# Row fetches, gate matrix layout and modulation sums in a two-layer block with PEER experts

## The chip, the cores and the metric

The kernel runs on one core of a Trainium2 chip, in one launch. The metric is the device time of one execution in microseconds; the shown time is the median of three runs. Five engines take part: TensorE (PE; its weight loads are PEld), VectorE (DVE), ScalarE (ACT), GpSimd (POOL) and SyncE (SP), which here mainly issues DMAs. Each engine works through its own list of instructions in order; semaphores hold an instruction until what it needs is there.

## The reference

Two blocks in a row on x of 256 tokens by 1024, in float32. The first has two layers of [mixer, PEER expert layer], each with adaptive norms; the second, a twice repeated [swiglu, hybrid mixer, swiglu], isn't touched by the change. What matters here is the first block:

```python
def first_block(...):
    for layer in range(2):
        sh1, sc1, g1, sh2, sc2, g2 = split(cond @ ada_w[layer] + ada_b[layer], 6)      # 1024 x 6144
        csh1, csc1, cg1, csh2, csc2, cg2 = split(cond_ctx @ ada_w[layer] + ada_b[layer], 6)
        h, hc = modulate(rmsnorm(x), sh1, sc1), modulate(rmsnorm(ctx), csh1, csc1)
        y, yc = even_mixer(h, hc) if layer == 0 else odd_mixer(h, hc)                  # MLA
        x = x + g1 * y
        x = x + g2 * peer_ffn(modulate(rmsnorm(x), sh2, sc2), ...)
        if layer == 0:
            ctx = ctx + cg1 * yc
            ctx = ctx + cg2 * peer_ffn(modulate(rmsnorm(ctx), csh2, csc2), ...)

def peer_ffn(h, w_q, sub_keys, u_tab, v_tab):       # 128 x 128 experts, 8 heads, 16 chosen per head
    s = einsum(h @ w_q, sub_keys)                   # scores against two sets of 128 keys
    expert, gate = top16 of the sums of the two top-16 lists; gate = softmax
    act = gelu(einsum('td,thkd->thk', h, u_tab[expert]))
    return einsum('thk,thkd->td', gate * act, v_tab[expert])
```

The twelve modulation vectors of a layer (shift, scale and gate for the mixer and for the expert layer, each for x and for the context) are sums over the 1024 rows of ada_w. In layer 1 the context is wanted only as input of the mixer, so of the context's vectors only the first two are used there.

## The kernel before

Tokens lie in tiles of 128: layer 0 has four (two of x, two of the context), layer 1 two. Every float32 product is three matmuls of a high and a low part (L311, L312, L313, the helper `mm3`); a weight slab is cast on ScalarE (L342, `wh`) and its rest is taken on VectorE (L316, `wl`). All elementwise helpers have one line each: L316 two tensors, L325 multiply and add with a column (`stt`), L320 a tensor and a scalar.

**PEER layer.** `peer_route` computes scores, the top 16 and a dense gate matrix: for every token its weight for each of the 16384 experts. `gbuild` makes it for 32 tokens at a time in a staging tile (tag T16: two of them in layer 0, one in layer 1; ScalarE writes it at L1310) and L1314 writes it to DRAM, 2 MB per 32 tokens, 12 writes in layer 0 and 8 in layer 1. It is laid out as [32-token block][row][all experts]. Beside it, twelve of the 32 chunks get their hidden part u made ahead (`pre`, 1, 4, 6, 9, 12, 14, 17, 20, 22, 25, 28, 30) and stored in `ud`. Then come the chunks of 512 experts: u_part multiplies the tokens by a chunk of the u table (or reads `ud`), applies the gate, for which the chunk's slice of the gate matrix is read back at L1376 (`t<-gd`, 768 KB in layer 0, 512 KB in layer 1), and v_tiles multiplies by the chunk of the v table. V of chunk c-1 follows U of chunk c.

**Layer 0** (`peer_mixed`, 950 to 1885 us) does three token tiles so, 384 columns wide. The fourth, tile 0, is done by fetching rows: 128 steps fetch for each token one row of the u table (`pur`, L1442 on GpSimd, an indirect DMA of 512 KB) and multiply it by the token's vector on VectorE (L1447); 128 steps fetch rows of the v table (`pvr`) and add them up (L325, 128x1024). The fetches share five buffers (tag GR). A counter (`rate`) says after how many matmul groups the next fetch is written.

**Modulation sums.** `ada_thread` makes them 512 columns at a time: an accumulator is cleared on GpSimd (L470), the bias is loaded into its first row (L472), eight pieces of ada_w of 128x512 are multiplied by a column of the condition and added on VectorE (L325, 128x512), for x and the context, and TensorE sums over the partitions (L308). In layer 0's chunks stand the fourteen blocks that are left by then: columns 10 and 11 of layer 0, and all twelve of layer 1, 56 loads of 512 KB (L1586). Blocks 4 to 11 of layer 1 only need x, so one sum per piece.

**What follows.** `tail` adds a finished token tile to the residual (loaded at L1595, `t<-rd`) and makes the norm of layer 1. The first projection of MLA follows (`mwa`, `mwb`, result `pm`), then the attention by heads (scores, softmax on VectorE and ScalarE with L607 and L609, values) and the output projection (`mwo`), then route 1, and the dense chunks of layer 1 (`peer_dense`).

**The order.** The program's text sets dependences and priorities, but a list scheduler fixes each engine's order ahead of the run; pools of buffers (`T4`, `raw`, `GR`) limit how early a load may stand. DMAs on SP are in one queue list: a load that waits for a buffer holds all later ones.

## Time and profile before

| | us |
|---|---|
| median of three runs (4143.91 to 4156.93) | 4145.16 |
| profiled execution | 4154.18 |
| its span, first to last instruction | 4152.4 |
| TensorE busy | 3949.9 (95%) |
| VectorE busy | 2978.3 (72%) |
| ScalarE busy | 1910.5 (46%) |
| GpSimd busy | 748.4 (18%) |

Stages on its time axis: layer 0's mixer to about 627 us, its route to 950, its chunks with row fetches to about 1885, the transition with the first projection to 1965, the attention and output projection to 2065, route 1 to 2300, the dense chunks of layer 1 to 2860, the second block to the end. A share of busy time is a mean over stages: TensorE's 95% says that most stages wait for it, and the windows say which do not. An idle engine matters only where TensorE waits for it.

### The profile page before, as it was taken

Reading aid. Unit: us, or ns where it says so; the run is one execution under the profiler, and the core shown is the slowest. Engines: PE = TensorE matmul, PEld = TensorE weight load, DVE = VectorE, ACT = ScalarE, POOL = GpSimd, SP = SyncE. Lnnn points to the kernel's source line nnn. Section 1 sums busy time; section 2 is a strip of 40 time slices with the busy share of each in tenths; the row PEclk is TensorE's granted clock in tenths of the full one; section 3 lists DMA queues with packets and bytes.
Section 4 is the critical chain, followed back from the end, with each engine's and each line's share of the span. In section 5 each row is a group of like instructions: output and inputs, shape, how many; then the busy total and the mean of one; then the engine's idle time right before and its main releaser. Section 6 shows DMA issues by size and latency. Waiting matters only on the chain.

```text
span 4152.4 us, 63830 instructions
## 1 busy us (share of the span) xinstructions
PE 3949.9 (95%) x24927; PEld 3558.4 (86%) x24927; DVE 2978.3 (72%) x5618; ACT 1910.5 (46%) x3241; POOL 748.4 (18%) x579
## 2 busy tenths in 40 slices
PE   8999999998999999999999999999999999999999
PEld 5877888897888778888789988888989998989988
DVE  4468579986998889847699556656667766567765
ACT  3344344772333233335558544444554454444444
POOL 2133302113444556300131000000010000000000
PEclk9999999999999999999999999999999999999999
DMA  4222133669999999843247866665545455445443
GB/s 169 92 84 79 44 141 111 221 253 327 353 363 353 354 373 369 328 162 123 97 162 277 288 221 227 242 221 190 182 169 188 179 178 178 173 168 183 174 172 142
DMA packets 234974, 862.66 MB, mean 208 GB/s; under 512 B 18944, under 2 KB 116096, under 8 KB 164528
## 3 DMA queue, kind: packets, MB, share of 16 engines
q1 hardware_dynamic: 197808, 724.35, 49.0%
q0 software_dynamic: 36864, 134.23, 8.5%
q8 instruction: 195, 3.19, 0.3%
q14 instruction: 107, 0.88, 0.1%
HBM read 795.97 MB, written 62.55 MB: 207 GB/s over the span
## 4 chain that ended last, share of the span: by engine, by line
PE 54%; DVE 16%; DMA 8%; issue 3%; ACT 1%; POOL 1%; SPq 0%; DVEq 0%; POOLq 0%; ACTq 0%
PE p L311 17%; PE p L313 17%; PE p L312 17%; DVE t L316 5%; DVE t L325 4%; DVE wl L316 3%; DMA t<-in_pvr,c 2%; DMA w<-in_pv 2%; DMA t<-in_ada_w 2%; PE p L308 2%; DVE t L1447 1%; PE p L435 1%; POOL t L1442 1%; DMA w<-ud 1%; DMA t<-in_pur,c 0%
## 5 line engine op out<-in xcount | busy, mean ns | idle before, releaser
L316 DVE TENSOR_TENSOR wl<-w,wh 128x1024 fp32r<-128x1024 f32 (+1 forms) x933 | 1132.1, 1219 | 704.7 <-ACT wh L342 682.6
L342 ACT CAST wh<-w 128x1024 fp32r<-128x1024 f32 x1017 | 1057.8, 1047 | 999.8 <-PE p L312 430.0
L311 PE MATMUL p<-t,wh 128*128 128x256 f32 (+2 forms) x4784 | 1460.1, 305 | 17.9 <-ACT wh L342 4.5
L313 PE MATMUL p<-t,wl 128*128 128x256 f32 (+2 forms) x4784 | 1450.1, 303 | 5.2 <-DVE wl L316 3.3
L312 PE MATMUL p<-t,wh 128*128 128x256 f32 (+2 forms) x4784 | 1449.5, 303 | 1.4 <-DVE t L316 1.4
L311 PEld LDWEIGHTS p<-t,wh 128*128 128x128 f32 x4784 | 921.7, 193 | 39.1 <-ACT wh L342 6.9
L313 PEld LDWEIGHTS p<-t,wl 128*128 128x128 f32 x4784 | 921.5, 193 | 19.3 <-DVE wl L316 5.1
L312 PEld LDWEIGHTS p<-t,wh 128*128 128x128 f32 x4784 | 921.9, 193 | 17.0 <-DVE t L316 1.7
L312 PE MATMUL p<-wl,t 128*128 128x512 f32 (+3 forms) x2134 | 818.0, 383 | 25.7 <-DVE wl L316 24.8
L311 PE MATMUL p<-wh,t 128*128 128x512 f32 (+3 forms) x2134 | 817.8, 384 | 21.6 <-ACT t L401 11.4
L313 PE MATMUL p<-wh,t 128*128 128x512 f32 (+3 forms) x2134 | 815.0, 383 | 8.0 <-DVE t L316 6.1
L316 POOL TENSOR_TENSOR wl<-w,wh 128x1024 fp32r<-128x1024 f32 x84 | 220.2, 2632 | 1983.1 <-ACT wh L342 1714.0
L312 PEld LDWEIGHTS p<-wl,t 128*128 128x128 f32 x2134 | 410.3, 192 | 100.8 <-DVE wl L316 29.9
L311 PEld LDWEIGHTS p<-wh,t 128*128 128x128 f32 x2134 | 409.9, 192 | 100.3 <-ACT t L401 13.8
L313 PEld LDWEIGHTS p<-wh,t 128*128 128x128 f32 x2134 | 408.2, 192 | 89.4 <-DVE t L316 10.8
L316 DVE TENSOR_TENSOR t<-t,t 128x256 f32<-128x256 f32 (+10 forms) x732 | 352.9, 487 | 64.6 <-ACT t L401 42.3
L325 DVE SCALAR_TENSOR_TENSOR t<-t,c,t 128x512 f32<-128x512 f32 (+2 forms) x367 | 328.1, 920 | 44.9 <-DMA t<-in_ada_w 20.9
L401 ACT CAST t<-t 128x256 fp32r<-128x256 f32 (+3 forms) x314 | 138.7, 446 | 363.4 <-DVE t L316 363.4
L308 PE MATMUL p<-t,t 128*128 128x128 f32 (+3 forms) x1536 | 226.0, 301 | 1.9 <-DVE t L325 1.9
L1442 POOL DMA_INDIRECT t<-in_pvr,c x128 | 199.2, 1556 | 156.2 <-DVE t L325 127.7
L1442 POOL DMA_INDIRECT t<-in_pur,c x128 | 171.4, 1339 | 240.4 <-DVE c L1447 198.5
L308 PEld LDWEIGHTS p<-t,t 128*128 128x128 f32 (+1 forms) x1536 | 193.1, 192 | 25.0 <-issue 11.3
(200 smaller groups left out, 3004.5 us busy)
## 6 DMA issues: line engine op xcount, KB each, us to landing
w<-in_pu SPq DMA_DIRECT2D x128, 1024.0 KB
w<-in_pv SPq DMA_DIRECT2D x128, 1024.0 KB
w<-in_fgu SPq DMA_DIRECT2D x88, 1024.0 KB
w<-in_hin SPq DMA_DIRECT2D x48, 1024.0 KB
w<-in_fdn SPq DMA_DIRECT2D x44, 1024.0 KB
gd<-t SPq DMA_DIRECT2D x20, 2048.0 KB
t<-in_ada_w SPq DMA_DIRECT2D x56, 512.0 KB
t<-gd SPq DMA_DIRECT2D x32, 768.0 KB
```

What stands on the lines that cost most here:

```text
L308: nc.tensor.matmul(o, l, r, start=first, stop=last)
L311: nc.tensor.matmul(o, l[0], r[0], start=first, stop=False)
L312: nc.tensor.matmul(o, l[0], r[1], start=False, stop=False)
L313: nc.tensor.matmul(o, l[1], r[0], start=False, stop=last)
L316: return (e or nc.vector).tensor_tensor(o, a, b, op)
L325: nc.vector.scalar_tensor_tensor(o, a, s, b, op0=op0, op1=op1)
L342: i = nc.scalar.copy(hi[:, :m], raw[:, s : s + m])
L401: nc.scalar.copy(dst[0], src)
L435: nc.tensor.transpose(o, i, ident[:n, :n])
L1442: nc.gpsimd.indirect_dma_start(r, None, src, at)
L1447: nc.vector.tensor_tensor_reduce(r, r, xr, 1.0, 0.0, ALU.mult, ALU.add, act[:, s : s + 1])
```

## The change

Three things change.

1. Of the fourteen blocks of modulation sums in layer 0's chunks only six stay: columns 10 and 11 of layer 0, and 0 to 3 of layer 1. Columns 4 and 5 are made during the first projection of layer 1, 6 to 9 during its attention, 10 and 11 during its dense chunks. In the latter two places the pieces come as loads of 1 MB through the ring of raw weight slabs (`ada_raws`), and the accumulator has a tag of its own (AD).
2. The gate matrix in DRAM is laid out as [chunk][row][32-token block x 128]. A chunk's slice is now one run of 6 KB (layer 0) or 4 KB (layer 1) per partition, where it was twelve or eight runs of 512 B; a write of 32 tokens becomes 32 runs of 512 B per partition, where it was one of 16 KB.
3. The row fetches' rate is reckoned to the end of chunk 31, and what is left of them and the fetched tile's `tail` are written before the last token tile of chunk 31 instead of before the whole of it. One normed tile takes a buffer of tag T6 instead of GR.

```diff
     def ada_thread(blocks, acc_tag, row_tag, raws):
         for l, n, c0 in blocks:
-            acc = T(acc_tag, [P, 2, 512])
-            nc.gpsimd.memset(acc[:, c0:, :], 0.0)
+            a2 = T(acc_tag, [P, 2 - c0, 512])
+            acc = {c: a2[:, c - c0, :] for c in range(c0, 2)}
+            nc.gpsimd.memset(a2, 0.0)
...
+    def ada_raws(l, n):
+        for kh in range(2):
+            w = load(A["ada_w"][l, 2 * n + kh])
+            for k in range(4):
+                yield w[:, k * 512 : (k + 1) * 512]
...
             if g2 == 3:
-                nc.sync.dma_start(gd[tb], st[0].rearrange("p a b -> p (a b)"))
+                o = gd.rearrange("c p (b e) -> b p c e", e=P)[tb]
+                nc.sync.dma_start(o, st[0].rearrange("p (c a) b -> p c (a b)", a=4))
...
-                nc.sync.dma_start(HG[c, "g"], gd[:, :, HS(c)].rearrange("b p e -> p b e"))
+                nc.sync.dma_start(HG[c, "g"], gd[c].rearrange("p (b e) -> p b e", e=P))
...
-    def peer_dense(l, cols, nt, gd, ud, pre):
+    def peer_dense(l, cols, nt, gd, ud, pre, side):
...
+            next(side, None)
             u_part(c, 1)
...
-        rate = 2 * P / (4 + 30 * (4 + 2 * nt)) * 1.0001
+        rate = 2 * P / (4 + 31 * (4 + 2 * nt) + 4) * 1.0001
...
-        for _ in got:
-            pass
-        for n in range(2):
-            tail(0, n, acc0[:, n * 512 : (n + 1) * 512])
         Ws = [v_slab(31, hf) for hf in range(2)]
         for t in range(nt):
+            if t == nt - 1:
+                for _ in got:
+                    pass
+                for n in range(2):
+                    tail(0, n, acc0[:, n * 512 : (n + 1) * 512])
             for hf in range(2):
-                v_tiles(31, hf, Ws[hf], [t])
+                v_tiles(31, hf, Ws[hf], [t], step)
...
-        gd = pdr.tile([12, P, 4096], F32, tag="gd", name="gd0")
+        gd = pdr.tile([32, P, 12 * P], F32, tag="gd", name="gd0")
...
-            ab = [(0, 10, 0), (0, 11, 0)] + [(1, n, n > 3) for n in range(12)]
+            ab = [(0, 10, 0), (0, 11, 0)] + [(1, n, 0) for n in range(4)]
...
+                        hT[t] = Pair("T6" if t else "GR", [P, 8, P]), 0
...
+            ad = ada_thread([(1, n, 1) for n in (4, 5)], "T4", "T2", raws)
...
                     nc.scalar.copy(pm[:, t, c0 : c0 + w], ps[:, :w])
+                    for _ in range(2):
+                        next(ad, None)
...
+        ad = ada_thread([(1, n, 1) for n in range(6, 10)], "AD", "T2", ada_raws)
...
         for h in range(8):
             p = scores(h)
+            next(ad, None)
             if prev is not None:
                 list(attend(h - 1, prev))
+            next(ad, None)
...
-        gd = pdr.tile([8, P, 4096], F32, tag="gd1", name="gd1")
+        gd = pdr.tile([32, P, 8 * P], F32, tag="gd1", name="gd1")
...
-        with phase("D2", T8=4, T4=4):
-            y = dense()
+        with phase("D2", T8=4, T4=4, AD=1):
+            y = dense(ada_thread([(1, n, 1) for n in (10, 11)], "AD", "T2", ada_raws))
```

Where the instructions stand on three engines follows, at the places that matter.

VectorE in layer 0, between the two halves (`wl`) of the same slab of the v table, the 41st, in chunk 20; `t_9004` is the sum of the fetched rows, `t_14091` a modulation sum. Before:

```order
L316 TENSOR_TENSOR wl_13825<-w_13822,wh_13824 128x1024
L325 SCALAR_TENSOR_TENSOR t_9004<-t_14159,c_9084,t_9004 128x1024
L325 SCALAR_TENSOR_TENSOR t_14091<-t_14162,c_78,t_14091 128x512
L325 SCALAR_TENSOR_TENSOR t_9004<-t_14209,c_9084,t_9004 128x1024
L325 SCALAR_TENSOR_TENSOR t_14091<-t_14162,c_78,t_14091 128x512
L325 SCALAR_TENSOR_TENSOR t_9004<-t_14242,c_9084,t_9004 128x1024
L325 SCALAR_TENSOR_TENSOR t_14091<-t_14297,c_78,t_14091 128x512
L316 TENSOR_TENSOR wl_13829<-w_13822,wh_13828 128x1024
```

The same place now:

```order
L316 TENSOR_TENSOR wl_13646<-w_13643,wh_13645 128x1024
L325 SCALAR_TENSOR_TENSOR t_9004<-t_14982,c_9084,t_9004 128x1024
L325 SCALAR_TENSOR_TENSOR t_9004<-t_14997,c_9084,t_9004 128x1024
L325 SCALAR_TENSOR_TENSOR t_9004<-t_15040,c_9084,t_9004 128x1024
L325 SCALAR_TENSOR_TENSOR t_9004<-t_15073,c_9084,t_9004 128x1024
L316 TENSOR_TENSOR wl_13650<-w_13643,wh_13649 128x1024
```

The three multiply-adds of the sums are gone, and a fourth fetched row stands in their place. Over the whole stage the last fetched row is added about when chunk 24's v slabs are split, where it was chunk 26.

SP in the attention of layer 1, its list of DMAs; `in_muq` are weights of the queries, `in_mwo` of the output projection, `in_pq` of route 1. Before:

```order
L334 DMA w_16980<-in_muq 128x1536
L1641 DMA c_16624<-in_rope 128x256
L334 DMA w_17038<-in_muq 128x1536
L334 DMA w_17497<-in_mwo 128x2048
L334 DMA w_17507<-in_mwo 128x2048
L334 DMA w_17593<-in_mwo 128x2048
L334 DMA w_17603<-in_mwo 128x2048
L334 DMA w_17733<-in_pq 128x2048
```

Now, from the second load of muq:

```order
L334 DMA w_16899<-in_muq 128x1536
L334 DMA w_16933<-in_ada_w 128x2048
L334 DMA w_17006<-in_ada_w 128x2048
L334 DMA w_17064<-in_ada_w 128x2048
L334 DMA w_17163<-in_ada_w 128x2048
L473 DMA t_17003<-in_ada_b 1x512
L334 DMA w_17221<-in_ada_w 128x2048
L334 DMA w_17308<-in_ada_w 128x2048
L473 DMA t_17160<-in_ada_b 1x512
L334 DMA w_17366<-in_ada_w 128x2048
L334 DMA w_17433<-in_mwo 128x2048
```

Seven loads of ada_w (the eighth stands before muq) now stand between muq and mwo in the same ring of raw slabs.

VectorE in the attention; the reductions, L609 or L616 (reciprocals) and 128x512 scalings are the softmax of one query tile after the other. Before:

```order
L609 RECIPROCAL t_17111<-t_17109 128x1
L1735 TENSOR_REDUCE t_17120<-p_17114 128x1
L320 TENSOR_SCALAR t_17108<-t_17108,t_17111 128x512
L320 TENSOR_SCALAR t_17122<-t_17120 128x1
L609 RECIPROCAL t_17127<-t_17125 128x1
L1735 TENSOR_REDUCE t_17136<-p_17130 128x1
L320 TENSOR_SCALAR t_17124<-t_17124,t_17127 128x512
```

Now:

```order
L616 RECIPROCAL t_16994<-t_16992 128x1
L1753 TENSOR_REDUCE t_17016<-p_17010 128x1
L320 TENSOR_SCALAR t_16991<-t_16991,t_16994 128x512
L320 TENSOR_SCALAR t_17018<-t_17016 128x1
L325 SCALAR_TENSOR_TENSOR t_17003<-w_17006,c_78,t_17003 128x512 x2
L616 RECIPROCAL t_17023<-t_17021 128x1
L1753 TENSOR_REDUCE t_17032<-p_17026 128x1
L320 TENSOR_SCALAR t_17020<-t_17020,t_17023 128x512
```

Two multiply-adds of the sums now stand ahead of a reciprocal, in the place where VectorE waits for ScalarE's exponentials.

## Rows read from the trace of the kernel before

**Rows 1.** Windows of the stages, core 0; the first row names the columns.
```profile
core 0: us, PE busy (x) PEld busy (x) DVE busy (x) ACT busy (x) POOL busy (x), PEclk, DMA share, GB/s
950.00:1380.00 430.00, 406.71 (x1973) 356.07 (x1972) 387.00 (x588) 139.04 (x192) 183.04 (x140) 0.98 0.96 354
1380.00:1600.00 220.00, 200.75 (x972) 176.28 (x971) 191.35 (x223) 69.25 (x97) 116.31 (x72) 0.97 0.97 366
1600.00:1740.00 140.00, 131.13 (x606) 111.51 (x605) 123.70 (x122) 42.84 (x59) 80.38 (x58) 0.96 0.98 367
1740.00:1885.00 145.00, 145.00 (x714) 129.39 (x714) 68.11 (x84) 53.94 (x73) 0.00 (x0) 1.00 0.49 170
```

**Rows 2.** Chain of waits by line, 1380 to 1600 and 1600 to 1740 us.
```profile
by line: DMA t<-in_ada_w 28.0%; DMA t<-in_pvr,c 17.8%; issue 17.6%; DVE t L325 10.5%; DMA w<-ud 9.0%; DVE wl L316 6.3%; POOL t L1442 6.2%; DVE t L316 5.2%; DVE w L316 2.3%; POOL t L470 0.4%; DVE t L320 0.3%; SPq L1586 0.2%; SPq L334 0.1%; D
...
by line: DMA t<-in_pvr,c 42.1%; issue 24.6%; POOL t L1442 11.5%; DVE t L325 7.3%; DVE wl L316 5.5%; PE p L312 2.6%; PE p L313 2.3%; PE p L311 2.2%; DVE t L316 2.1%; POOLq L1442 0.1%; DVEq L325 0.1%; DVEq L316 0.0%
```

**Rows 3.** Instructions by form, VectorE and TensorE, 950 to 1740: count, busy us, mean ns, idle before.
```profile
...
L325 DVE SCALAR_TENSOR_TENSOR t<-t,c,t 128x1024 f32<-128x1024 f32 x126 | 161.5, 1282 | 20.8 <-DMA t<-in_pvr,c 19.5
L325 DVE SCALAR_TENSOR_TENSOR t<-t,c,t 128x512 f32<-128x512 f32 x160 | 114.3, 747 | 20.9 <-DMA t<-in_ada_w 20.9
...
L312 PE MATMUL p<-wl,t 128*128 128x512 f32 x612 | 245.8, 402 | 24.8 <-DVE wl L316 24.8
L312 PE MATMUL p<-t,wh 128*128 128x384 f32 x533 | 180.0, 338 | 0.0
```

**Rows 4.** TensorE by form from 1740 to 1885, and its chain: start, us, what.
```profile
...
L311 PE MATMUL p<-wh,t 128*128 128x512 f32 x132 | 51.4, 389 | 0.0
...
L311 PE MATMUL p<-t,wh 128*128 128x384 f32 x106 | 35.5, 335 | 0.0
...
1745.52 0.23 PE p L311
```

**Rows 5.** DMA traffic and issues from 950 to 1740 us.
```profile
DMA packets 102831, 283.95 MB, mean 359 GB/s; under 512 B 7067, under 2 KB 50459, under 8 KB 91959
...
q0 software_dynamic: 36864, 134.23, 44.8%
...
t<-in_ada_w SPq DMA_DIRECT2D x56, 512.0 KB
```

**Rows 6.** Windows inside dense layer 1 and inside the second block.
```profile
2350.00:2800.00 450.00, 450.00 (x2685) 402.77 (x2684) 269.39 (x367) 221.91 (x328) 0.00 (x0) 1.00 0.67 229
3550.00:3700.00 150.00, 150.00 (x1059) 141.40 (x1058) 81.95 (x106) 69.48 (x88) 0.00 (x0) 1.00 0.53 188
```

**Rows 7.** Windows from layer 0 to route 1, one chain step, VectorE groups 1930 to 2065.
```profile
1885.00:1930.00 45.00, 40.99 (x224) 36.11 (x222) 33.91 (x86) 26.46 (x67) 0.00 (x0) 0.96 0.22 69
1930.00:1965.00 35.00, 33.38 (x162) 27.93 (x161) 31.46 (x82) 19.69 (x36) 1.62 (x6) 1.00 0.45 159
1965.00:2030.00 65.00, 65.00 (x337) 49.99 (x336) 36.96 (x92) 37.85 (x78) 0.00 (x0) 1.00 0.18 64
2030.00:2065.00 35.00, 26.01 (x134) 21.55 (x134) 22.71 (x43) 14.25 (x31) 13.14 (x6) 0.85 0.36 138
...
1877.30 9.35 DMA t<-rd
...
L320 DVE TENSOR_SCALAR t<-t,t 128x512 f32<-128x512 f32 x20 | 11.4, 578 | 0.1
...
L609 DVE RECIPROCAL t<-t 128x1 f32<-128x1 f32 x16 | 2.6, 164 | 15.5 <-ACT t L607 15.5
```

**Rows 8.** Route 1: window, the gate writes (first and last start), ScalarE waits, chain step.
```profile
2230.00:2300.00 70.00, 70.00 (x720) 69.27 (x719) 56.90 (x69) 58.36 (x135) 10.88 (x4) 1.00 0.83 301
...
L1314 SPq DMA_DIRECT2D gd<-t x8: 319/320/320, 2173.7 to 2298.6; - x8
...
ACT t L1310 <- DMA gd<-t: 2.6, 3, 1.3
...
2191.80 11.76 DMA gd<-t
```

More of the change, by code (lines that the diff above doesn't have):

```diff
@@ L468, in ada_thread @@
         for l, n, c0 in blocks:
-            acc = T(acc_tag, [P, 2, 512])
-            nc.gpsimd.memset(acc[:, c0:, :], 0.0)
+            a2 = T(acc_tag, [P, 2 - c0, 512])
+            acc = {c: a2[:, c - c0, :] for c in range(c0, 2)}
+            nc.gpsimd.memset(a2, 0.0)
             for c in range(c0, 2):
-                nc.sync.dma_start(acc[0:1, c, :], A["ada_b"][l : l + 1, n * 512 : (n + 1) * 512])
+                nc.sync.dma_start(acc[c][0:1, :], A["ada_b"][l : l + 1, n * 512 : (n + 1) * 512])
             for k, w in enumerate(raws(l, n)):
                 for c in range(c0, 2):
-                    stt(acc[:, c, :], w, cact[:, k, c : c + 1], acc[:, c, :], ALU.mult, ALU.add)
+                    stt(acc[c], w, cact[:, k, c : c + 1], acc[c], ALU.mult, ALU.add)
                 if k % 2:
@@ L482, in ada_thread @@
                 if c0:
-                    mm(po[:1, :], ones1[:, 0:1], acc[:, 1, :])
+                    mm(po[:1, :], ones1[:, 0:1], acc[1])
                 else:
-                    mm(po[:2, :], ones1[:, 0:2], acc[:, 0, :], True, False)
-                    mm(po[:2, :], ones1[:, 1:3], acc[:, 1, :], False, True)
+                    mm(po[:2, :], ones1[:, 0:2], acc[0], True, False)
+                    mm(po[:2, :], ones1[:, 1:3], acc[1], False, True)
                 ro = T(row_tag, [2, 512])
@@ L492, in ada_thread @@
                     for c in range(c0, 2):
-                        mm(po[:, 2 * q + c : 2 * q + c + 1], acc[:, c, HS(q)], ones1[:, 0:1])
+                        mm(po[:, 2 * q + c : 2 * q + c + 1], acc[c][:, HS(q)], ones1[:, 0:1])
                 ada_put(l, n, po, c0)
@@ L1133, in peer @@
             return lambda *a: peer_mixed(l, cols, nt - off, gd, ud, pre, *a)
-        return lambda: peer_dense(l, cols, nt, gd, ud, pre)
+        return lambda side: peer_dense(l, cols, nt, gd, ud, pre, side)
     def peer_route(l, hT, nt, gd, ud, pre, late_tile, off):
@@ L1588, in raws @@
                         yield w[:, k * 512 : (k + 1) * 512]
-            ab = [(0, 10, 0), (0, 11, 0)] + [(1, n, n > 3) for n in range(12)]
-            hT = []
+            ab = [(0, 10, 0), (0, 11, 0)] + [(1, n, 0) for n in range(4)]
+            hT = {}
             gb = []
@@ L1605, in tail @@
                 if n == 1:
-                    if t < 2:
-                        hT.append((Pair("GR", [P, 8, P]), 0))
-                    elif t == 2:
+                    if t == 2:
                         p = Pair("HG", [P, 8, 256])
-                        hT.extend([(p, 0), (p, 1)])
+                        hT[2], hT[3] = (p, 0), (p, 1)
+                    elif t < 2:
+                        hT[t] = Pair("T6" if t else "GR", [P, 8, P]), 0
                     mod_tile(R, t, 1, 0, t // 2, hT[t][0], "T4", hT[t][1])
@@ L1628, in peer0 @@
                     nc.scalar.copy(pm[:, t, c0 : c0 + w], ps[:, :w])
+                    for _ in range(2):
+                        next(ad, None)
+            for _ in ad:
+                pass
             tap("pm", pm)
@@ L1635, in mla @@
     def mla(R, pm):
-        with phase("C", T16=2, T8=4, T4=3, Q4=2, K4=2):
+        with phase("C", T16=2, T8=4, T4=3, Q4=2, K4=2, AD=1):
             return mla_body(R, pm)
@@ L1722, in mla_body @@
                 split((qn[:, 4 * s + c, :], qo[s][:, c, :]), ps[:, :256])
+                if c % 2:
+                    next(ad, None)
         yT = Pair("T8", [P, 8, 256])
@@ L1755, in mla_body @@
             p = scores(h)
+            next(ad, None)
             if prev is not None:
                 list(attend(h - 1, prev))
+            next(ad, None)
             prev = p
+        for _ in ad:
+            pass
         X = R[:, 2:4, :]
```

## The prediction

> **What bounds the kernel now.** I began with the windows of the page's stages [rows 1]. While PEER layer 0 runs with row fetches, 950 to 1740 us, the DMA engines are busy 0.96 to 0.98 of the time, and TensorE is not: 406.71 + 200.75 + 131.13 = 738.6 us busy of 790. As soon as the fetches are over (1740 to 1885) TensorE is busy all 145 us and the DMA share is 0.49. The granted clock is 0.96 to 1.00 in all four rows, so it is not the throttle. The chain of waits of the same stretches [rows 2] names the same thing: from 1380 to 1600 the largest piece is the load of ada_w (28.0%), then the fetched rows of pvr (17.8%); from 1600 to 1740 the pvr rows are 42.1%, and the matmuls hardly appear. VectorE is second: 387.00 + 191.35 + 123.70 = 702 us of 790, 0.89.
>
> How much TensorE loses there I worked out from its own pace. In the chain a 512-column matmul follows the last after 0.23 us [rows 4], so the 132 triples between 1740 and 1885 are 132 x 3 x 0.23 = 91 us, and the other 54 of the 145 us go to 106 triples of 384 columns, 0.51 us each. From 950 to 1740 it has 612 and 533 triples [rows 3]: 612 x 0.69 + 533 x 0.51 = 694 us; with 10 for the 112 small matmuls of the sums, 704. It took 790. So **some 85 us are lost in this stage, and no change to it can give back more**. In the dense stage of layer 1 (2350 to 2800) TensorE is busy all 450 us with a DMA share of 0.67 [rows 6]: nothing is to be won there.
>
> **Part 1, the modulation sums leave layer 0.** Of 14 blocks 8 go. The 56 loads of 512 KB [rows 5] become 24: 32 x 0.524 = 16.8 MB less. At 359 GB/s, the rate of this stretch [rows 5], that is 47 us of DMA time. VectorE loses 64 multiply-adds of 128x512 at 747 ns [rows 3], 48 us.
>
> **Part 2, the gate matrix stored by chunk.** Its 768 KB per chunk arrive in runs of 6 KB instead of twelve of 512 B. The trace has no such read, so I bound it. In the dense stage of layer 1, which reads the old layout, 229 GB/s cost a share of 0.67; in the second block 188 GB/s cost 0.53 [rows 6]. At the latter's price 229 GB/s would cost 0.646, so over 450 us 0.024 x 450 = 11 us go to about 26 chunk reads of 512 KB (the stage's 32 chunks take from 2310 to 2860), 0.42 us each, 0.6 us for 768 KB. With the rounding of the shares it is 0.4 to 1.0. For 25 chunks 15 us (10 to 25). Nothing in the rows makes the longer run the dearer one, so the range ends at 0 below.
>
> The Trainium skill (DMA: Bandwidth & Descriptors, Specifications) puts line rate at transfers of 512 B and more, which would make part 2 worth nothing on the reads. The two rows speak for a small difference; by that page of the Trainium skill this term is 0, which makes the sum -24 for the stage; that case is the second rival.
>
> **Part 3, the row fetches.** The rate per step falls from 0.842 to 0.805 and the drain moves behind most of chunk 31. But a list scheduler places the instructions, and in the order that is built the fetches do not spread: the last multiply-add of a fetched row stands two chunks earlier on VectorE (about chunk 24, before 26), because where a multiply-add of the sums stood, the next fetched row moves up. So the DMA work of two more chunks falls behind the end of the fetches. All traffic of 950 to 1740 is 283.95 MB [rows 5]; without 134.23 MB of fetches (the software queue) and 29.4 MB of ada_w 120 MB stay for some 27 chunks, 4.5 MB each, so two chunks are 9 MB, 25 us.
>
> **The sum for this stage.** DMA busy from 950 to 1740: 0.96 x 430 + 0.97 x 220 + 0.98 x 140 = 763 us. Less 0.97 x 47 = 45, 15 and 25: 678 us. At the same share of 0.967 that takes 701 us. TensorE needs 704 - 50 (two chunks: each has 3 tiles x 2 halves x 4 = 24 triples of 0.69; one of the two also 4 x 8 = 32 of 0.51, since the other's u was made ahead) = 654; VectorE has 702 - 48 - 23 (two chunks at the 0.47 of 1740 to 1885) = 631, 0.90 of 701, as crowded as before. So DMA still ends last, and 701 + 50 us of the two chunks at TensorE's pace are 751 in place of 790: **-39 us**. Bounds: at a share of 0.93 (the earlier fetches wait more for VectorE) 729 + 50, -11; at full use of the DMA engines 678 + 50, -62; TensorE's own pace ends it at -85, which would need both other engines to vanish.
>
> **What the moves cost.** (a) Transition and first projection, 1885 to 1965: TensorE busy 74.4 of 80 us, VectorE 65.4 [rows 7]. Sixteen multiply-adds come in at 0.65 us (between 0.58, a 128x512 operation of this place in [rows 7], and the crowded 0.75), 10 us, ahead of norms and weight splits that TensorE waits for. The new order also starts with the tiles that the dense path makes, while before the fetched tile was ready early: the residual arrives 9.35 us after its issue at 1877.30, and its tail ran beside chunk 31. I take +8, between 0 (all in VectorE's 15 us of gaps) and 15. (b) Attention of layer 1, 1965 to 2065: 32 multiply-adds, 20 us. VectorE's gaps behind the exponentials are 16 of 15.5 us in all [rows 7], and one or two sums fit in each; what does not fit lengthens a chain in which TensorE is busy all 65 us up to 2030. The sums' loads take the slots of the raw ring ahead of mwo, so the output projection's weights come after the attention instead of beside it: four weights of 128x2048 and their eight splits. I take half of the 20 us as hidden: +9 (0 to 18). Queued behind the waiting loads on SP are mwo and the first pq, and route 1's start waits for those. (c) Dense layer 1: 16 multiply-adds in a stage with 0.40 of VectorE free, two rows of matmuls, +2 (0 to 6).
>
> (d) Writing the gate matrix. A write of 2 MB was 128 runs of 16 KB and becomes 4096 of 512 B. In route 0 two staging tiles lie between; no wait on a write shows there, 0. In route 1 there is one. Eight writes go from 2173.7 to 2298.6, 17.8 us apart in the mean; ScalarE waits only 2.6 us in three times for them [rows 8], though one stands in the chain for 11.76 us. So the landing ends almost exactly when the tile is wanted, and what is added waits: ScalarE, whose queue holds the weight casts and the u activations that TensorE wants. DMA is already 0.83 busy there. No row prices a 512 B write: from below 0 (as cheap as now), from above the 11.76 us once more for each of seven writes, 80 us, of which TensorE's four result tiles ahead of this activation and ScalarE's idle 12 of 70 us swallow some. The nearest row is the read of part 2, where small pieces cost 0.42 us in 512 KB, 1.7 us in 2 MB; seven times 1.7 is 12, and a little is absorbed: **+10 (0 to 35)**.
>
> Total: -39 + 8 + 9 + 2 + 10 = -10. The profiled execution took 4154.18 us (span 4152.4), 9 us above the median of the runs; the sum is made on its trace, so 4144 for it, and I carry the difference to the median: 4145.16 - 10, about **4135**.
>
> **The rivals.** First, **the stage loses nearly all waits**: fetches, sums and gate runs were in each other's way, and without them the DMA engines run full (-62). With moves that cost 20, 4103. For it: 42.1% and 28.0% of the chain are exactly these waits. Against: VectorE's 0.90 stays.
>
> Second, **no measurable change**: small runs cost nothing more on reads, and the fetches that moved up are bound by VectorE, -20; the moves cost 24: 4149. For it: the last pvr rows wait for VectorE's adds as much as for DMA. By the page of the Trainium skill named in part 2 the time would come out here.
>
> Third, **slower**: route 1 with its one staging tile. If a write lands 5 us later than now, seven writes are +35, and with +20 from the other moves and -30 in layer 0 that is +25, 4170. It decides from about 3 us of delay per write: at -30 + 20 + 7 x 3.2 the sum passes the 12.4 us that a measurement can tell from no change (0.3%). For it: the landing just in time, DMA at 0.83. Against: by the nearest row a write grows by 1.7 us only. The Trainium skill (DMA: Bandwidth & Descriptors, Latency and other measured facts) has 207 GB/s at a row pitch of 512 KiB against 214 unhindered; by that page the pitch of the new pieces in layer 1 (512 KB) would add next to nothing, and no run here shows it.
>
> That the change does not do what it says is so in one part already and is in the sum: the fetches end earlier, not at the last chunk.
>
> **How the numbers follow.** Forecast 0.46, first rival 0.22, second 0.18, third 0.14. The forecast's own spread (4120 to 4150) puts 0.2 of its 0.46 below 4132.7. Faster: 0.20 + 0.22 = 0.42. Slower: 0.11 from the third and 0.04 from the second, 0.15. Within 0.3%: 0.43. The range of 8 in 10 reaches the first rival at 4104 and comes short of the third at 4165: half of the first (0.11) and two thirds of the third (0.09) are left out.
>
> **What would show it.** Right: the last fetched row lands some 195 us before the stage's end at its last chunk, where it was 145 (1740 to 1885); DMA share still 0.95 or more up to there; layer 0 about 39 us shorter; TensorE waits of 5 to 10 us each in the projection and the attention; ScalarE's wait for the gate write in route 1 about 1 to 2 us per write. Wrong: a DMA share well under 0.93 with VectorE over 0.95 (the moved-up fetches are bound by VectorE); gate writes that stand in the chain for 15 us each; or an attention in which TensorE waits over 20 us.

## The result and the profile after

The changed kernel takes **4183.72 us** in the median of four runs (4179.13 to 4185.94) against 4144.67, also of four, of the kernel before: ratio 1.0073, 95% interval 1.006 to 1.0086. The two medians by themselves would give 1.0094; against the medians of the kernel before in the later groups of runs, 4151.87 to 4152.95, 4183.72 is 1.0074 to 1.0077. The changed kernel is slower by some 30 us, and outside the range on record. The profiled executions differ by 24.7 us (spans 4177.1 and 4152.4), and the account below is made on these two.

To see where the time came from, the two traces are cut at five events that every version has. In the changed kernel these rows (the instructions of one tile or line: durations in ns, first and last start in us) give them: the last fetch of a v row, the load of the residual, the first and the last reduction of the softmax, the first and the last write of the gate matrix in route 1.

```profile
L1451 POOL DMA_INDIRECT t<-in_pvr,c x128: 933/1300/2617, 1350.4 to 1656.7; - x128
...
L1605 SPq DMA_DIRECT2D t<-rd x1: 327/327/327, 1866.1 to 1866.1; - x1
...
L1753 DVE TENSOR_REDUCE t<-p x16: 670/671/692, 1983.0 to 2031.7; 128x1 f32<-128x512 f32 x16
...
L1322 SPq DMA_DIRECT2D gd<-t x8: 370/370/534, 2188.0 to 2319.9; - x8
```

The kernel before has 1729.4, 1877.3, 1977.4 and 2016.4, 2173.7 and 2298.6 for the same events. The differences between events are the stages:

| stage | before, us | after, us | difference |
|---|---|---|---|
| start to the residual's load (all up to the end of layer 0's chunks) | 1877.3 | 1866.1 | -11.2 |
| to the first softmax (transition, projection) | 100.1 | 116.9 | +16.8 |
| to the last softmax (attention) | 39.0 | 48.7 | +9.7 |
| to the first gate write (output projection, start of route 1) | 157.3 | 156.3 | -1.0 |
| to the last gate write (route 1) | 124.9 | 131.9 | +7.0 |
| to the end | 1853.8 | 1857.2 | +3.4 |
| span | 4152.4 | 4177.1 | +24.7 |

The costs are near what was forecast (29 us, 37 measured). The gain is not: 39 us were forecast and 11 came. The windows of the changed kernel that answer to [rows 1] and [rows 7]:

```profile
core 0: us, PE busy (x) PEld busy (x) DVE busy (x) ACT busy (x) POOL busy (x), PEclk, DMA share, GB/s
950.00:1380.00 430.00, 403.66 (x1972) 355.06 (x1970) 383.58 (x576) 142.26 (x194) 190.91 (x147) 0.98 0.94 358
1380.00:1600.00 220.00, 200.16 (x943) 174.43 (x942) 193.65 (x199) 66.22 (x94) 128.41 (x89) 0.96 0.95 357
1600.00:1740.00 140.00, 135.01 (x657) 118.92 (x656) 94.39 (x100) 47.37 (x64) 36.10 (x27) 1.00 0.72 269
1740.00:1885.00 145.00, 144.82 (x707) 128.11 (x706) 66.30 (x91) 51.74 (x70) 0.00 (x0) 1.00 0.45 157
1885.00:1930.00 45.00, 33.80 (x190) 30.01 (x189) 36.47 (x83) 24.10 (x58) 1.51 (x3) 0.89 0.41 137
1930.00:1965.00 35.00, 28.19 (x125) 22.43 (x125) 30.61 (x78) 19.05 (x39) 1.72 (x6) 0.90 0.47 172
1965.00:2030.00 65.00, 62.67 (x331) 47.85 (x329) 50.49 (x117) 30.16 (x66) 1.58 (x3) 1.00 0.34 123
```

Up to 1600 us TensorE is as idle as before (603.8 us busy of 650, before 607.5), although 16.8 MB of ada_w are gone and the gate matrix is read in long runs. The DMA share fell only from 0.96 and 0.97 to 0.94 and 0.95. What changed is the traffic: from 1315 to 1660 the old kernel's VectorE added 94 rows of the v table and 52 pieces of the sums, the new one 124 rows and no sum. These rows of the two traces (groups of VectorE by form from 1315 to 1660; the last column is idle time just ahead and what ended it; first the kernel before, then after) show the price:

```profile
L325 DVE SCALAR_TENSOR_TENSOR t<-t,c,t 128x1024 f32<-128x1024 f32 x94 | 120.4, 1281 | 11.5 <-DMA t<-in_pvr,c 10.7
L325 DVE SCALAR_TENSOR_TENSOR t<-t,c,t 128x512 f32<-128x512 f32 x52 | 38.9, 748 | 20.9 <-DMA t<-in_ada_w 20.9
```

```profile
L325 DVE SCALAR_TENSOR_TENSOR t<-t,c,t 128x1024 f32<-128x1024 f32 x124 | 159.1, 1283 | 37.7 <-DMA t<-in_pvr,c 35.8
L1456 DVE CUSTOM_DVE_ANT_0 t<-t,t 128x1024 f32<-128x1024 f32 x17 | 20.4, 1220 | 5.7 <-DMA t<-in_pur,c 5.6
```

VectorE's 20.9 us of waiting for ada_w have gone, and its 10.7 us of waiting for fetched rows have become 35.8 (41 with the last rows of the u table). A weight split for TensorE that stands behind such an add waits with it: TensorE's wait for `wl` in this stretch rose (waits of TensorE: total us, times, longest; before, then after):

```profile
PE p L312 <- DVE wl L316: 16.9, 8, 6.8
...
PE p L312 <- DVE wl L316: 28.1, 14, 5.5
```

The landing of one row did not get slower: 8.2 us in the median after, 8.8 before. So I read it that the rows didn't queue longer for the DMA engines; they were asked for too late. A fetch needs one of five buffers (GR), and a buffer is held from the fetch's issue until the add. From 1315 to 1650 the new kernel issued 140 fetches, one in 2.4 us; if all five buffers are in use, each is held 12 us, of which the landing is 8.2 and GpSimd's issue 1.4. From 1315 to 1660 GpSimd stood 95.0 us waiting for adds that free a buffer; but in the kernel before it stood 100.4 us, so that wait alone does not tell the two apart. That is my theory S: the denser order of fetches ran into the ring of five, and freed DMA time could not be used. The rival D is the prediction's own reading, that bytes and DMA time bound the stage, and the gain was lost in some other way. Rival T puts the projection's loss on the new order of the tails and not on the sums; rivals W and B are two causes for route 1.

### The profile page after: what moved, and what is told of

It reads as the page before. It is cut to its first block, busy times and chain, and to the rows that moved or that the text cites. A ratio compares the mean times of both kernels' runs of the same rounds, so it can differ in the third digit from the quotient of the medians.

```text
span 4177.1 us, 63835 instructions
## 1 busy us (share of the span) xinstructions
PE 3947.5 (95%) x24927; PEld 3554.9 (85%) x24927; DVE 2977.0 (71%) x5618; ACT 1912.3 (46%) x3241; POOL 730.1 (17%) x579
## 4 chain that ended last, share of the span: by engine, by line
PE 50%; DVE 7%; DMA 2%; ACT 1%; issue 1%; POOL 0%; DVEq 0%; SPq 0%; ACTq 0%; POOLq 0%
PE p L311 16%; PE p L313 16%; PE p L312 16%; DVE t L316 2%; DVE t L325 2%; DMA gd<-t 1%; DVE wl L316 1%; PE p L308 1%; PE p L435 1%; ACT t L1317 0%; DVE t L320 0%; DMA t<-in_pvr,c 0%; ACT wh L342 0%; DVE t L1167 0%; DVE t L1169 0%
## 5 line engine op out<-in xcount | busy, mean ns | idle before, releaser
L311 PE MATMUL p<-wh,t 128*128 128x512 f32 (+3 forms) x2134 | 818.6, 384 | 20.2 <-ACT t L401 8.5
L325 DVE SCALAR_TENSOR_TENSOR t<-t,c,t 128x512 f32<-128x512 f32 (+2 forms) x319 | 296.1, 945 | 44.6 <-DMA t<-in_pvr,c 38.4
L1451 POOL DMA_INDIRECT t<-in_pvr,c x128 | 181.9, 1421 | 126.1 <-DVE t L325 95.0
```

The lines of the kernel that those rows point to most:

```text
L311: nc.tensor.matmul(o, l[0], r[0], start=first, stop=False)
L325: nc.vector.scalar_tensor_tensor(o, a, s, b, op0=op0, op1=op1)
L1451: nc.gpsimd.indirect_dma_start(r, None, src, at)
```

## The experiments

All are compared with the kernel before on the same chip (its medians there were 4152.23, 4151.87 and 4152.95 us for the three groups). The stage differences in the table are against the profiled execution of before in the cut above. Each is one execution: e1, e2 and e7 have the same code up to the residual's load and show -5.8, -11.8 and -12.9 there, the projection of unchanged code lies between -1.5 and +4.2, and the last column moves by 2 us with the same code. Differences below these are not read.

| run | ratio, 95% interval | layer 0 | projection | attention | output proj. | route 1 | rest |
|---|---|---|---|---|---|---|---|
| changed kernel | 1.0073 (1.006 to 1.0086) | -11.2 | +16.8 | +9.7 | -1.0 | +7.0 | +3.4 |
| e1 gate matrix, both layers | 1.0007 (0.9996 to 1.0019) | -5.8 | +0.3 | 0.0 | -0.1 | +6.5 | +0.4 |
| e2 gate matrix, layer 0 | 0.9977 (0.9967 to 0.9987) | -11.8 | +4.2 | 0.0 | +1.2 | +0.8 | +0.7 |
| e3 sums moved | 1.0047 (1.0033 to 1.0061) | -11.2 | +12.8 | +9.7 | -1.0 | +0.2 | +3.4 |
| e4 fetch rate and tails | 1.0037 (1.0025 to 1.0048) | +1.2 | +6.3 | 0.0 | +0.8 | -1.1 | +2.2 |
| e5 changed, six buffers | 1.0004 (0.9992 to 1.0016) | -39.7 | +17.5 | +9.6 | -1.0 | +8.1 | +2.3 |
| e6 changed, four buffers | 1.0174 (1.0157 to 1.0191) | +38.1 | +17.8 | +9.7 | -0.9 | +6.7 | +4.6 |
| e7 as e1, two staging tiles | 1.0005 (0.9995 to 1.0015) | -12.9 | -0.2 | 0.0 | +1.3 | +5.6 | +3.0 |
| e8 as e2, fetches paced | 1.0011 (1.0001 to 1.002) | +3.0 | +1.6 | 0.0 | +1.2 | -1.1 | +2.3 |
| e9 before, six buffers | 0.998 (0.9968 to 0.9992) | -10.5 | -1.1 | 0.0 | +0.9 | -1.2 | +2.3 |
| e10 as e2, six buffers | 0.9933 (0.992 to 0.9945) | -32.0 | -1.2 | 0.0 | +1.0 | -1.1 | +2.3 |
| e11 six of the sums moved, six buffers | 0.9961 (0.9946 to 0.9976) | -34.4 | -1.5 | +9.6 | -0.9 | -1.1 | +4.8 |
| e12 all sums moved, none in the projection, six buffers | 1.0023 (1.0014 to 1.0032) | -33.4 | -2.1 | +9.9 | +28.7 | -1.0 | +6.1 |

### The parts one by one (e1 to e4)

e1 takes the four edits of the gate matrix alone (the two tiles, L1314 and L1376, as in the change's diff). e2 takes them in layer 0 only:

```diff
-                nc.sync.dma_start(gd[tb], st[0].rearrange("p a b -> p (a b)"))
+                if l == 0:
+                    o = gd.rearrange("c p (b e) -> b p c e", e=P)[tb]
+                    nc.sync.dma_start(o, st[0].rearrange("p (c a) b -> p c (a b)", a=4))
+                else:
+                    nc.sync.dma_start(gd[tb], st[0].rearrange("p a b -> p (a b)"))
```

> The kernel before with the gate matrix stored by chunk in both layers, nothing else; the order of VectorE and of the fetches is that of before. Theory S (the stage of layer 0 is bound by the ring of five fetch buffers, so freed DMA time buys little; the writes cost in route 1): layer 0 shorter by 0 to 6 us, route 1 longer by 7 us, dense layer 1 +-1, sum +1 to +7, the same within 0.3%. Rival D (DMA time is the bound of layer 0, as the prediction reckoned): layer 0 shorter by 15 us, route 1 +7, sum about -8.

> The gate matrix by chunk in layer 0 alone; layer 1 keeps the old layout, so route 1 writes runs of 16 KB. Theory S: layer 0 shorter by 0 to 6 us, route 1 as before, sum -6 to 0. Rival D: -15. In both the difference to the run with both layers is the price of route 1's writes of 512 B: 7 us by the trace of the changed kernel; if it is under 2 us, route 1 lost its 7 us to something else (later loads of pq).

e3 takes the change without the gate matrix and without the edits in `peer_mixed` and in the tails; e4 takes those edits alone:

```diff
-        rate = 2 * P / (4 + 30 * (4 + 2 * nt)) * 1.0001
+        rate = 2 * P / (4 + 31 * (4 + 2 * nt) + 4) * 1.0001
...
-        for _ in got:
-            pass
-        for n in range(2):
-            tail(0, n, acc0[:, n * 512 : (n + 1) * 512])
         Ws = [v_slab(31, hf) for hf in range(2)]
         for t in range(nt):
+            if t == nt - 1:
+                for _ in got:
+                    pass
+                for n in range(2):
+                    tail(0, n, acc0[:, n * 512 : (n + 1) * 512])
```

> The eight blocks of modulation sums moved out of layer 0, gate matrix and fetch code as before. Theory S: the fetches move up and layer 0 is shorter by 5 to 12 us; the projection stage +8 to +18, the attention +9, dense layer 1 +3, sum +10 to +25. Rival D: layer 0 shorter by 25 us or more, sum about -5 to +5. Rival T (the projection's loss is from the order of the tails in the last chunk and not from the sums): projection +0 to +4, sum +0 to +10.

> The lower fetch rate, the drain and the fetched tile's tail behind most of chunk 31, and the tag of the second normed tile; sums and gate matrix as before. Theory S: the built order has the last fetch at the same chunk as before, layer 0 +-2; projection +0 to +5; sum -2 to +6. Rival T: projection +10 to +17, sum +10 to +17.

The gate matrix alone is worth 6 to 13 us in layer 0 (e1, e2, e7). Two of the three are near D's 15 and above what S had allowed, e1's 5.8 is within S: in the kernel before, DMA time does count. The sums alone are worth 11.2 us there, far from D's 25. And the two don't add: the change has both and gains 11.2. Once the sums are out, the cheaper reads are worth nothing that shows (e3 and the changed kernel: the same -11.2, where executions of one code differ by 7). That is what a limit other than DMA time looks like. The projection's loss is 12.8 us from the sums and 6.3 from the tails, so T holds for a third of it; the 6.3 lie only 2 above what unchanged code can show, but one wait in the trace, shown further down, belongs to the tails. As a whole e4 is 10 to 20 us slower by its ratio, as T had it (10 to 17) and not S (-2 to +6); its profiled execution has only 9.4 of that, and the rest is not placed. Route 1's loss comes with the new layout in layer 1: 6.5 us with it (e1), 0.8 without (e2).

### The ring of five (e5, e6)

```diff
-        with phase("B2", HG=3, T6=2, T4=4, XR=1, AC=1, GR=5):
+        with phase("B2", HG=3, T6=2, T4=4, XR=1, AC=1, GR=6):
```

(e6: `GR=4`.)

> The changed kernel with six buffers for fetched rows in place of five; the order of the fetches on VectorE stays as it was. In the changed kernel VectorE waits 41 us between 1315 and 1660 us for fetched rows that have not landed, and the weight splits behind them hold TensorE 28 us. Theory S (the ring of five bounds the fetches: 140 in 335 us, 2.4 us each, five buffers of 12 us from issue to release): layer 0 shorter by 5 to 15 us, the rest unchanged, sum -5 to -15 against the changed kernel (4183.72). Rival D (DMA time bounds them, share 0.96): -2 to +2.

> The changed kernel with four buffers for fetched rows, the order of the fetches as it was but for one row. Theory S: a ring of four gives a fetch every 3 us at best, the end of the fetches comes 40 to 100 us later and layer 0 is longer by 20 to 60 us. Rival D: the DMA engines stay as full, +0 to +8.

One more buffer gives the changed kernel 28.5 us in layer 0, more than I expected, and one less costs 49.3. The order on VectorE is the same with six as with five; with four a few instructions stand some places away. The rows of VectorE, TensorE's wait for weight splits and the windows from 1315 to 1660, first with six, then with four, and last the window with five:

```profile
L325 DVE SCALAR_TENSOR_TENSOR t<-t,c,t 128x1024 f32<-128x1024 f32 x127 | 162.9, 1282 | 16.6 <-DMA t<-in_pvr,c 14.4
...
PE p L312 <- DVE wl L316: 11.3, 6, 3.6
...
1315.00:1660.00 345.00, 329.31 (x1596) 288.50 (x1596) 316.82 (x342) 113.73 (x160) 205.99 (x139) 1.00 0.96 372
```

```profile
L325 DVE SCALAR_TENSOR_TENSOR t<-t,c,t 128x1024 f32<-128x1024 f32 x104 | 133.3, 1282 | 56.6 <-DMA t<-in_pvr,c 55.3
...
PE p L312 <- DVE wl L316: 35.2, 11, 6.5
...
1315.00:1660.00 345.00, 292.77 (x1318) 249.48 (x1317) 268.62 (x296) 94.94 (x131) 178.55 (x126) 0.93 0.87 323
```

```profile
1315.00:1660.00 345.00, 312.98 (x1475) 271.87 (x1474) 299.71 (x320) 103.12 (x144) 202.41 (x143) 0.97 0.96 358
```

The wait for rows is 14.4 us with six buffers, 35.8 with five and 55.3 with four, TensorE's wait for weight splits is 11.3, 28.1 and 35.2, and its busy time in these 345 us is 329.3, 313.0 and 292.8. With four buffers even the landing is quicker (7.1 us in the median), and still all waits longer. D falls for the changed kernel, S stands.

### Route 1 with two staging tiles (e7)

```diff
-        with phase(f"R{l}", T16=2 if nt == 4 else 1, T8=2 if nt == 4 else 3, T4=3, T1=6, TG=1, M=4, UA=2):
+        with phase(f"R{l}", T16=2, T8=2 if nt == 4 else 3, T4=3, T1=6, TG=1, M=4, UA=2):
```

> The gate matrix by chunk in both layers as in the run with that alone, and a second staging tile in route 1. Theory W (a write of 512 B runs lands later and ScalarE, with one tile, waits for it): route 1 is as long as with the old layout, -5 to -8 against the run with one tile, sum -4 to -8 against before. Rival B (the DMA engines are full in route 1, and the write's own time is the price): route 1 stays 4 to 7 us longer.

W falls: with two tiles ScalarE no longer waits for the gate write, and route 1 is still 5.6 us longer. Its waits from 2060 to 2330 us (total, times, longest), first with one tile (e1), then with two:

```profile
ACT t L1310 <- DMA gd<-t: 13.0, 6, 3.9
ACT t L1339 <- DMA ud<-t: 5.9, 3, 3.9
```

```profile
ACT t L1339 <- DMA ud<-t: 23.7, 10, 6.1
```

The wait has moved to the write of the u activations, which shares the engines. The windows from 2225 to 2295, first of the kernel before, then of e1:

```profile
2225.00:2295.00 70.00, 70.00 (x707) 69.27 (x705) 59.97 (x72) 58.45 (x136) 14.88 (x6) 0.98 0.83 299
```

```profile
2225.00:2295.00 70.00, 64.85 (x663) 63.68 (x662) 49.04 (x69) 56.29 (x130) 17.08 (x5) 1.00 0.90 282
```

A share of 0.83 carried 299 GB/s, and 0.90 carries 282. That is 2.8 us of DMA time per MB before and 3.2 with the short runs: some 8 us more for the 19.74 MB of this window, 2 us for each of its four writes. In the same window the changed kernel, e5, e6 and e7 give 3.2 too, and the kernels with the old layout in layer 1 2.7 to 2.9. It fits B, a price in DMA time.

### Fetches paced to their chunk (e8)

The change says that the fetches are spread to the last chunk, and the built order does the opposite. To see what spreading would give, e8 loads the indices of a chunk's fetches into a slot of that chunk's buffer of hidden values:

```diff
-                HG[c] = T(thg, [P, 4, 2, Tn], F32R)
+                h = T(thg, [P, 8 * Tn + 32], F32R)
+                HG[c] = h[:, : 8 * Tn].rearrange("p (a b t) -> p a b t", a=4, b=2)
+                paced["t"], paced["base"] = h[:, 8 * Tn :].bitcast(I32), count[0]
...
+                nc.sync.dma_start(paced["t"][:, :m], gi[:, a : a + m])
...
-            at = bass.IndirectOffsetOnAxis(ap=ix[:, s : s + 1], axis=0)
+            at = bass.IndirectOffsetOnAxis(ap=paced["t"][:, o : o + 1], axis=0)
```

> The kernel with the gate matrix by chunk in layer 0 alone, and the row fetches paced: the indices of each chunk's fetches are loaded into that chunk's buffer of hidden values, of which there are three, so that a fetch can't run ahead of its chunk; in the built order the last fetched row is added at chunk 30 instead of 26. Theory S (bunched fetches are what TensorE loses by): layer 0 shorter by a further 15 to 45 us than in the run without pacing, sum -20 to -50 against before. Rival D (the bytes of layer 0 need their time wherever they stand; 763 + 71 us of DMA time in 935): -10 to +5 against the run without pacing.

The run is some 14 us slower than without pacing (1.0011 against 0.9977), all of it in layer 0, which neither S nor D had. The fetches did spread, the last one is issued at 1827.9 us, but the row of VectorE from 1315 to 1660 shows a new wait:

```profile
L325 DVE SCALAR_TENSOR_TENSOR t<-t,c,t 128x1024 f32<-128x1024 f32 x76 | 97.3, 1280 | 36.4 <-DMA t<-in_pvr,t 35.9
```

35.9 us for 76 rows: a fetch may not start before its chunk's buffer is free, and its add, as I read it, stands on VectorE's list closer behind than the landing takes. If so, this is no fair test of spreading: a pace that takes away the lead of a fetch over its add would cost like a ring that is too small. That was not tested by itself. What an even spread with the full lead would give stays open.

### Towards a better version (e9 to e12)

e9 is the kernel before and e10 that of e2, each with `GR=6`. e11 is e10 with the sums 6 to 9 in the attention and 10 and 11 in the dense chunks of layer 1, as in the change, but 4 and 5 left in layer 0; e12 has 4 and 5 in the attention too:

```diff
-        ad = ada_thread([(1, n, 1) for n in range(6, 10)], "AD", "T2", ada_raws)
+        ad = ada_thread([(1, n, 1) for n in range(4, 10)], "AD", "T2", ada_raws)
```

> The kernel before with six buffers for fetched rows and nothing else. Theory S as it stands after the runs with six and four buffers (in the changed kernel the fetches stand closer and the ring of five bounds them; in the kernel before DMA time bounds them): layer 0 shorter by 0 to 8 us, sum -8 to 0. Rival R (the ring of five bounds layer 0 in every kernel): layer 0 shorter by 20 us or more.

> The gate matrix by chunk in layer 0 alone, with six buffers. Theory S: the DMA time that the reads give back (11 us with five) and little more, sum -10 to -18 against before. Rival R: -30 or more.

> The parts that the ledger prices well: gate matrix by chunk in layer 0 alone, six buffers, the sums 6 to 9 in the attention and 10 and 11 in dense layer 1; 4 and 5 stay in layer 0, fetch and tail code as before. Theory S: layer 0 -30 to -40 (with all eight blocks out it was -40), projection 0, attention +10, dense +3, sum -15 to -27. If the sums' price in layer 0 is not 3 to 4 us a block: -5 to -12.

> As the run before it, with 4 and 5 in the attention too, so that no sum is made in the projection. Theory Q (the projection lost by the loads of the sums, which stood on SP ahead of muqr and held it): projection 0 to +3 in place of the +13 of the run with the sums moved alone, attention +14 to +20, layer 0 a further 3 to 7 us shorter, sum -15 to -27. Rival V (the loss in the projection is VectorE's, 16 multiply-adds of 0.75 us in a stretch that is full): it goes along into the attention, +22 or more there.

**e10 beats both kernels**: 0.9933 of before (0.992 to 0.9945), a median of 4125.06 us. By the ratios the gate matrix gives 0.23% and the sixth buffer 0.20% when alone, and 0.67% together; S had 10 to 18 us and layer 0 alone gave 32.0, nearer to R's 30. R fails on e9, where it had 20 us or more for the buffer alone and 10.5 came. In layer 0 the sixth buffer is worth 10.5 us in the kernel before, 20.2 with the gate matrix by chunk (e10 against e2) and 28.5 with the whole change. VectorE's order is the same in the first two, so the denser order is not all of it. It looks as if both limits, DMA time and ring, are close to each other there and each hides part of the other's relief. The windows of e10 show DMA engines that carry more at nearly the same share, 385 GB/s at 0.98 where [rows 1] had 366 at 0.97:

```profile
950.00:1380.00 430.00, 414.02 (x2018) 363.71 (x2017) 396.12 (x600) 143.25 (x197) 191.03 (x145) 0.98 0.96 367
1380.00:1600.00 220.00, 210.97 (x1022) 186.01 (x1021) 203.62 (x231) 74.52 (x103) 127.95 (x80) 0.98 0.98 385
1600.00:1740.00 140.00, 135.76 (x671) 120.05 (x670) 122.49 (x129) 49.58 (x70) 64.85 (x44) 1.00 0.88 341
```

On top of that, taking six blocks of sums out of layer 0 is worth 2.4 us there (e11), less than executions differ, and costs 9.6 in the attention. The 3 to 4 us a block that I had read out of e5 are not there. So of the change only the layout in layer 0 is worth keeping.

e12 keeps the projection clean (-2.1), as Q had it, but this does not prove Q: the multiply-adds left the projection together with the loads. Layer 0 gains nothing further (Q had 3 to 7 us). The attention is no longer than with four blocks; but what did not fit is made after it, one multiply-add behind the other, and only then comes the first weight of the output projection. From its chain of waits:

```profile
2004.87 0.76 DVE t L325
2005.65 0.76 DVE t L325
2006.43 4.63 DMA w<-in_mwo
2011.09 1.05 ACT wh L342
```

This put 28.7 us on the output projection. Neither Q nor V had a loss there; V had one of this size, in the attention.

## Why the prediction was wrong, step by step

**The sum for layer 0 failed, at the step "At the same share of 0.967 that takes 701 us".** It took the DMA share for a measure of bytes and kept it constant. It had a limit for DMA, for VectorE and for TensorE, and none for the ring of five buffers that the moved-up fetches had to pass, which let one start every 2.4 us. The bytes came as forecast: 256.28 MB from 950 to 1665 us, at a share of 0.95, which is 679 us of DMA time where the sum had 678. But at that share they took 715 us and not 701 (with six buffers 255.42 MB took 685 us at 0.97), and the last fetch was issued 73 us earlier than before (1656.7 after 1729.4) where the sum had 89. The numbers that pointed to the limit were there to be read: a landing of 8.5 us for the rows of the u table and 8.8 for those of the v table, five buffers named in the code, and an order in which a fourth fetched row stands between the halves of a slab where there were three.

A second term was too small. Behind the last fetch stood 209.4 us up to the residual's load, where it was 147.9: 61.5 more, and not the 50 of two chunks. TensorE's matmuls behind the last add of a row say the same. These are the triples of 512 columns, before from 1740.5 to 1877, after from 1667.3 to 1866:

```profile
L312 PE MATMUL p<-wl,t 128*128 128x512 f32 x120 | 46.8, 390 | 0.0
...
L312 PE MATMUL p<-wl,t 128*128 128x512 f32 x180 | 70.4, 391 | 0.8 <-DVE wl L316 0.8
```

These are 60 triples more, at 24 a chunk two and a half chunks.

With a sixth buffer, and the same order on VectorE, the kernel gains 39.7 us in this stage, the 39 of the sum. What this shows is the ring: 28.5 us hung on one buffer. That the number agrees is luck. The last fetch is then issued at 1627.1, 102 us earlier than before, and 210.5 us stand behind it, 62.6 more; the two errors cancel. Nor is it the sum's mechanism, since e10, with all the sums still in layer 0, has 32.0 of these 39.7. Without part 2 the sum had 24 us, for the sums and the fetches that move up; beyond e10 there are 7.7, about as much as executions of one code differ.

**Part 2, the reads by chunk,** was right as long as the sums stay: 11.8 us in e2, 6 to 13 over the three runs, where 15 were put. The Trainium skill (DMA: Bandwidth & Descriptors, Specifications) puts line rate at transfers of 512 B and more. The runs do not bear this out for these reads of 512 B; [rows 6] had the better price. In the changed kernel, beside the ring, the gain does not show.

The sum's lower bound, -11 at a share of 0.93, is the number that came, with a share of 0.95. The reason given there, fetches that wait for VectorE, is half of what the runs show: the buffers come free by VectorE's adds, but VectorE was not full; it waited for rows.

**"0.90 of 701, as crowded as before" measured the wrong thing.** VectorE's busy time was as forecast, 0.89 from 950 to 1657 us; its idle time was spent ahead of rows that had not landed, with weight splits queued behind.

**(a) Transition and projection: +8 forecast (0 to 15), +16.8 measured.** The sums alone cost 12.8 (e3), the tails 6.3 (e4). TensorE's busy time in this stage grew by 4 us, from 94.5 to 98.7; the rest are waits, nearly all of them waits of its transposes (L435) for a normed tile (L320). From the residual's load to the first reduction of the softmax (1866.1 to 1983.0 in the changed kernel) they are, in the kernel before, the changed kernel, e3 and e4:

```profile
PE p L435 <- DVE t L320: 1.5, 3, 0.9
...
PE p L435 <- DVE t L320: 13.5, 3, 8.3
...
PE p L435 <- DVE t L320: 7.5, 3, 4.6
...
PE p L435 <- DVE t L320: 8.4, 2, 8.3
```

One wait of 8.3 us belongs to the tails: it stands in the four kernels that have their edit (changed, e4, e5, e6) and in none of the others. It was in the forecast as an idea without a term of its own: the norms of the four tiles run one behind the other, and the first no longer belongs to the fetched tile, which is ready early. The other, 5.1 us in the changed kernel and 4.6 in e3, belongs to the sums. The chain of the changed kernel leads to it over SP:

```profile
1920.38 3.59 DMA t<-in_ada_w
1924.10 0.75 DVE t L325
1924.85 0.87 DVE wl L316
1926.79 7.79 DMA w<-in_muqr
1934.60 1.15 ACT wh L342 x3
...
1936.16 0.57 ACT t L489
1936.73 1.61 ACT t L427 x8
1940.35 0.36 DVE t L320
1940.76 2.12 PE p L435 x8
```

The load of muqr stands on SP's list behind the loads of ada_w and lands late. ScalarE casts it, then copies the last sum (L489), and only then squares for the norms (L427) that TensorE waits for. But ScalarE was idle only 1.15 us for that load, so the 7.79 us are not its price. In SP's list these loads stand above the piece that is shown with the change, and I weighed only what was queued in the attention. How the 12.8 us divide between the loads, the 16 multiply-adds and their place on the lists no run separates.

**(b) Attention: +9 forecast, +9.7 measured**, with the same sums in the same gaps. The price that I put on the late loads of mwo is not there with four blocks (output projection -1.0) and is 28.7 us with six (e12).

**(c) Dense layer 1: +2 forecast; +3.4 in what follows route 1**, of which up to 2.3 is the difference between executions with the same code.

**(d) Gate write in route 1: +10 forecast (0 to 35), +7.0 measured**, and 2 us of DMA time for a write where 1.7 were taken from [rows 6]. The size was right and the place of the wait was not: the staging tile is no cause (e7), and the DMA engines' time fits what remains.

Of the rivals the third had the sign, by the wrong mechanism: route 1 lost 7 us and not 35. The miss of 35 us comes from a gain that did not arrive, 28 us of it, and 9 us more in the projection, less 2 us in the other stages. The sum of the measured stages is -11.2 + 16.8 + 9.7 - 1.0 + 7.0 + 3.4 = +24.7.

## What to carry to other kernels

Where transfers with a long way pass through a ring of buffers, the number of buffers divided by the time that one is held is a limit of its own (here five in 12 us, one fetch in 2.4 us), beside the bytes and the engines' busy time; reckon it before counting on freed DMA time, and look at the idle time ahead of the consumer for what ended it. Before moving work into a stage to relieve another, look at the whole list of the queue it joins: a load that waits for a slot holds the weights behind it. Test the parts of a change alone: here one part of three paid, 0.23% by itself and 0.67% together with a buffer that the change had not touched.

## What the runs showed of the hardware

The DMA engines' busy share is a poor measure of what is left: at a share of 0.96 the stretch from 1315 to 1660 us moved 358 GB/s in the changed kernel with five buffers and 372 with six, and from 1380 to 1600 e10 moved 385 at 0.98 where the kernel before moved 366 at 0.97. Reads in runs of 512 B cost a little more engine time per byte than long runs. In dense layer 1, from 2350 to 2800 us, the kernel before moved 229 GB/s at a share of 0.67 [rows 6], which is 2.9 us per MB; the changed kernel comes to 2.8:

```profile
2350.00:2800.00 450.00, 450.00 (x2678) 400.92 (x2677) 275.65 (x371) 222.53 (x325) 0.53 (x1) 1.00 0.68 245
```

So do e1, e5, e6 and e7, which read by chunk there, and all the others come to 2.9. Writes in runs of 512 B cost more as well: 3.2 us per MB against 2.8 in route 1's window. The landing of a fetched row (512 KB for the 128 tokens) took 7.1 us in the median with four buffers, 8.2 with five and 8.6 with six in the changed kernel, so each further buffer went with 1.1 and 0.4 us more.
